# A fused two-block kernel on one core: list stage spread over steps, mask chunks one per two steps, loads and stores over two queues

## The chip, the core and the metric

The kernel runs on one core of a Trainium2 chip. Times are microseconds (us) from the device; the metric is the time of the whole kernel, the median of several runs. Engines: PE is TensorE's matmul, PEld its weight load, DVE is VectorE, ACT ScalarE, POOL GpSimd, SP SyncE. SP, ACT and POOL also issue transfers; their issuing sides stand in the trace as SPq, ACTq and POOLq.

## The reference, cut to what matters

256 tokens with 2048 features pass two transformer-like blocks. What the change touches is the last part, a mixture of 128 x 128 = 16384 single-neuron experts. Every token picks 128 of them (8 heads, 16 each) and weighs them by a gate:

```
z   = einsum('cd,ced->ce', x, u[expert])       # hidden product of token and expert
act = gelu(z) * gate
x   = x + einsum('ce,ced->cd', act, v[expert]) # then a last rms norm
```

## The kernel before, in words

All weights arrive as items of 1 MB (128 partitions x 2048 floats) and are used once. `stream` (line 388) runs over all items in two halves each. For a half it emits: on ScalarE the rounded high part `whi` of a half that lies three halves ahead (`cut_hi`, 416), one call of `step`, on VectorE the rest `wlo` (`cut_lo`, 423; four `wlo` buffers, five `whi`), and the matmuls of the present half. `cut_lo` of an item's second half frees its raw buffer and issues the load of the item three further on, on SP's queue (`load`, 408). Each engine and each queue works in the order in which the program emits.

`step` (347) advances background tasks: of the first three of the list `tasks` each runs to its next `yield`. A yield names a cost; steps get a budget of 1.3 here, debt is carried over, and a task whose cost leaves the credit at or under zero ends the step. In this part each task advances by about one yield per step, with two steps per item.

In the expert part there are 16 items `w_pq` (the choice of experts), 128 items `peer_u` (hidden products with all experts, two items to a PSUM pair), one item `peer_v` by column and 105 gathered items of `peer_v`.

- Scatter (1360): POOL adds the gates one by one into a table `zg` in DRAM, first the first token tile's and then the second's, 256 transfers.
- Hidden products: at the end of a pair `post_u` (1590) copies one part of the PSUM pair on ScalarE (`scaled`, 337), adds the other on VectorE (340), multiplies (341), applies GELU on ScalarE (1594), and stores to the table on ScalarE's queue (1595). All of it is emitted at once behind the pair's last matmul.
- Masks: `mask_task` (1418) waits for item 63 (first token tile) or 96 (second). It reads the tile's gates back from the table in eight chunks of 1 MB on SP's queue (1427), behind the last scatter of that tile, into four buffers `vraw`; VectorE takes the maximum of a chunk (1445); for the second tile POOL halves the chunk first (1438).
- Lists: `list_task` (1457), which follows the second masks, builds a list of the experts in use, of three classes: scans and small matmuls, then 37 pieces in a loop (1556). For a piece POOL compares (`late`, 1516), VectorE makes a selection (`hot`, 1523), TensorE multiplies (1533) into one of two PSUM banks `bg1`, ScalarE takes signs (1542), and VectorE sums them (1548), one iteration apart each. The end (1564 to 1569) makes the indices and sets the flag "lists".
- Rows: items of `peer_v` are loaded by POOL with a gather by index (1649). `cut_lo` asks for them seven items ahead (430), and the first one runs steps until the flag is there:

```
while "lists" not in self.flags:
    self.step()
```

- End: `finish_tile` (1731) scales and stores the 256 x 2048 result in blocks of 512 columns: of the second tile blocks 0 to 2 on VectorE (1746), block 3 on ScalarE and POOL (1748, 1749), and all stores on SP (1750).

At the start `start`, `warm_up` and `prologue` (567 to 610) load the parameters and x in four parts and the first weights, all on SP.

Of the kernel before, what the change touches and what calls it, by code (L numbers as in the profile page):

```python
# [17 lines left out]
P = 128  # L18
# [39 lines left out]
LAST = 3  # L58
U_MASK = (63, 96)
EARLY = 3  # L60
# [187 lines left out]
class Build:  # L248
# [139 lines left out]
    def stream(self, items):  # L388


        n = len(items)
        raw, cut, order = {}, {}, []
        fills = {FILL_FROM + FILL_STEP * j: j for j in range(FILLS)}
# [25 lines left out]
        def cut_lo(k):  # L419
            if k < 2 * n:  # L420
                i, half = order[k]
                lo = self.strm.tile([P, HALF], F32R, name="wlo", tag="wlo", bufs=CUT_BUFS - 1)
                self.V.tensor_tensor(lo, raw[i][:, half * HALF:(half + 1) * HALF], cut[k][0].bitcast(F32),  # L423
                                     op=ALU.subtract)
                cut[k][1] = lo
                if half:
                    del raw[i]
                    if i + RAW_BUFS < n and not callable(items[i + RAW_BUFS][0]):
                        load(i + RAW_BUFS)
                    if i + RAW_BUFS + ROW_BUFS < n and callable(items[i + RAW_BUFS + ROW_BUFS][0]):  # L430
                        load(i + RAW_BUFS + ROW_BUFS)

# [134 lines left out]
    def start(self):  # L567
        nc, A, V = self.nc, self.A, self.V
        cp = self.constp
        self.x = cp.tile([P, KC, TOK], F32, name="xres")  # L570
        self.params = cp.tile([P, PARAM_N], F32, name="params")
        self.cons = {}
        self.ones = cp.tile([P, 1], F32, name="ones")
        self.keys = cp.tile([P, 2, P], F32, name="keys")
        self.decay = cp.tile([P, 2, KC], F32, name="decay")
        V.memset(self.ones, 1.0)
        self.zero = cp.tile([P, 2 * TOK], F32, name="zero")
        self.G.memset(self.zero, 0.0)
        self.warm_up()
        nc.sync.dma_start(self.params, A["params"])  # L580
        self.load_x(0)
        self.act = self.first = Operand(self)

    def warm_up(self):


        zero = self.rowp.tile([P, TOK], F32, name="rstd", tag="rstd", bufs=2)
        self.V.memset(zero, 0.0)
        w = self.strm.tile([P, HALF], F32R, name="wlo", tag="wlo", bufs=CUT_BUFS - 1)
        self.S.activation(w[:, :TOK], zero, AF.Copy)  # L590
        ps = self.bg1()
        for _ in range(WARM):
            self.T.matmul(ps[:, :TOK], w[:, :P], w[:, :TOK], start=True, stop=True)

    def load_x(self, i):
        self.nc.sync.dma_start(self.x[:, 4 * i:4 * i + 4], self.A["xT"][:, 4 * i:4 * i + 4])

    def prologue(self, load):
        load(0, 0, HALF)
        self.load_x(1)  # L600
        load(1, 0, HALF)
        self.load_x(2)
        self.load_x(3)
# [634 lines left out]
    def peer(self):  # L1238
# [144 lines left out]
        def begin_lists():  # L1383
# [17 lines left out]
            for name, (o, w) in offsets.items():  # L1401
                self.cons[name] = c3[:, o:o + w]
            st["abs"], st["gt"] = cut(2, PIECE * P), cut(2, PIECE, P)
            st["hot"], st["prer"] = self.t([2, PIECE * P], "hot", dt=F32R), self.t([PIECE, 3, 130], "pre", dt=F32R)
# [5 lines left out]
            st["zat"], st["vat"], st["over"] = cut(NLIST, dt=U32), cut(NLIST, dt=U32), cut(2, dt=mybir.dt.int32)  # L1410
            st["zg"], st["gates"], st["far2"], st["cd"] = cut(ROWS, 2, TOK), cut(TOK), cut(P + 4), [None, None]
            assert at[0] <= 2 * KC * TOK
# [5 lines left out]
        def mask_task(ti):  # L1418
# [23 lines left out]
            for g in range(8):  # L1442
                load(g + 3)
                half(g + 1)
                V.tensor_reduce(st["m"][:, ti, 16 * g:16 * g + 16], chunks[g], axis=AX.X, op=ALU.max)
                yield 1.25 if ti else 2.3
# [10 lines left out]
        def list_task():  # L1457
# [8 lines left out]
            yield 2.2  # L1466
            yield 0.0
            ps = self.bg1()
            T.matmul(ps[:, 0:3], self.con("tri"), st["n"], start=True, stop=True)
            yield 0.0  # L1470
            far = st["far2"]
            V.tensor_scalar(far[:, 0:3], ps[:, 0:3], -1.0, None, op0=ALU.mult)
# [7 lines left out]
            yield 2.0  # L1480
            yield 0.0
            ps = self.bg1()
# [19 lines left out]
            for c in range(3):  # L1502
# [5 lines left out]
                o += n  # L1508
            yield 1.4

# [26 lines left out]
            def signs(i):  # L1537
                if 0 <= i < len(pieces):
                    c, b, n = pieces[i]
                    col, pv = CLASS_AT[c] + b, banks.pop(i)  # L1540
                    S.activation(st["row"][:, col:col + n], pv[:, 0:n, P], AF.Copy)
                    S.activation(st["gt"][:, i % 2, 0:n], pv[:, 0:n, 0:P], AF.Sign, bias=self.con("past", col, col + 1))

            def sums(i):
                if i >= 0:
                    c, b, n = pieces[i]
                    col = CLASS_AT[c] + b
                    V.tensor_reduce(st["sum"][:, col:col + n], st["gt"][:, i % 2, 0:n], axis=AX.X, op=ALU.add)

            late(0)  # L1550
            late(1)
            yield 0.0
            yield 0.0
            hot(0)
            yield 0.0
# [34 lines left out]
        def post_u(i):  # L1590
            def f(ps):
                z = self.t([2, TOK], "z", 3)
                self.scaled(z, ps)
                S.activation(z, z, AF.Gelu)  # L1594
                d = self.nc.scalar.dma_start(table[:, i:i + 2, 0], z)
                for other in scatters[0] + scatters[1]:
                    self.tc.declare_no_dep(d.ins, other.ins, reason="gates stand beside the hidden products")
                stores.append(d)
            return f

        def post_last(j):

            def f(ps):
                if j == 0:
                    st["zlast"] = self.t([2, TOK], "z", 3)
                z = st["zlast"][:, j]
# [124 lines left out]
        def finish_tile(ti):  # L1731
# [11 lines left out]
            for fb in range(4):  # L1743
# [65 lines left out]
```

## Time and profile before

| | |
|---|---|
| time, median of 3 runs | 2501.93 us (2500.69 to 2504.32) |
| profiled execution | 2507.9 us, its span 2506.1 us |
| mean granted TensorE clock | 0.991 |
| busy | PE 98%, PEld 86%, DVE 71%, ACT 54%, POOL 32% |
| transfers | 548 MB, mean 219 GB/s |

The span is the time from the first to the last instruction of the profiled execution, cut into stretches in microseconds from its start. A granted clock of 1.00 is 2.4 GHz, 0.50 is 1.2 GHz; a value between is a mean over the stretch. The DMA share is the mean busy share of 16 transfer engines and can stand over 1, since packets overlap. In the waits, "A <- B: total, times, longest" says that A's engine sat idle until B.

### The profile page before, as it was taken

Reading aid. Unit: us, or ns where it says so; the run is one execution under the profiler, and the core shown is the slowest. Engines: PE = TensorE matmul, PEld = TensorE weight load, DVE = VectorE, ACT = ScalarE, POOL = GpSimd, SP = SyncE. Lnnn points to the kernel's source line nnn. Section 1 sums busy time; section 2 is a strip of 40 time slices with the busy share of each in tenths; the row PEclk is TensorE's granted clock in tenths of the full one; section 3 lists DMA queues with packets and bytes.
Section 4 is the critical chain, followed back from the end, with each engine's and each line's share of the span. In section 5 each row is a group of like instructions: output and inputs, shape, how many; then the busy total and the mean of one; then the engine's idle time right before and its main releaser. Section 6 shows DMA issues by size and latency. Waiting matters only on the chain.

```text
span 2506.1 us, 37010 instructions
## 1 busy us (share of the span) xinstructions
PE 2447.8 (98%) x14251; PEld 2146.4 (86%) x14251; DVE 1786.4 (71%) x2838; ACT 1342.8 (54%) x1881; POOL 805.0 (32%) x521
## 2 busy tenths in 40 slices
PE   9999999999999999999999999999979899999997
PEld 7888888898888888889999988888867788787885
DVE  7677777777666877766899755575567747777776
ACT  6566555555555677654444544444434535555555
POOL 0000000000000000000688877867523325565553
PEclk9999999999999999999999999999999899999999
DMA  7545555565544565654677777897785468899995
GB/s 251 187 152 173 197 206 202 187 226 185 196 150 165 202 198 186 219 191 170 171 193 196 218 221 208 222 314 223 219 263 189 147 246 299 318 316 320 317 320 183
DMA packets 179925, 548.00 MB, mean 219 GB/s; under 512 B 47585, under 2 KB 113633, under 8 KB 123938
## 3 DMA queue, kind: packets, MB, share of 16 engines
q1 hardware_dynamic: 102082, 391.18, 45.5%
q0 software_dynamic: 60384, 137.79, 19.3%
q10 hardware_dynamic: 17280, 16.65, 1.9%
q8 instruction: 112, 1.84, 0.3%
q14 instruction: 67, 0.55, 0.1%
HBM read 509.77 MB, written 35.78 MB: 218 GB/s over the span
## 4 chain that ended last, share of the span: by engine, by line
PE 84%; issue 4%; DVE 4%; DMA 3%; POOL 2%; ACT 2%; SPq 0%; ACTq 0%; POOLq 0%; DVEq 0%
PE mm L468 38%; PE mm L469 19%; PE mm L460 3%; PE mm L462 3%; PE mm L461 3%; PE bg L1695 2%; PE mm L1695 2%; PE mm L1696 2%; PE bg L1696 2%; PE mm L1694 2%; PE bg L1694 2%; DVE wlo L423 2%; POOL lists L1657 1%; DMA raw<-peer_u 1%; DMA vraw<-zg 1%
## 5 line engine op out<-in xcount | busy, mean ns | idle before, releaser
L468 PE MATMUL mm<-act,whi 128*128 128x512 f32 x4368 | 1228.2, 399 | 8.6 <-ACT whi L416 5.0
L423 DVE TENSOR_TENSOR wlo<-raw,whi 128x1024 fp32r<-128x1024 f32 x754 | 911.9, 1233 | 215.4 <-ACT whi L416 152.7
L468 PEld LDWEIGHTS mm<-act,whi 128*128 128x128 f32 x4368 | 792.9, 190 | 133.4 <-ACT whi L416 6.8
L1360 POOL DMA_INDIRECT zg<-sel,at x256 | 471.4, 1842 | 1316.8 <-DMA raw<-w_pq 1205.2
L416 ACT ACTIVATE whi<-raw 128x1024 fp32r<-128x1024 f32 x754 | 762.0, 1050 | 151.4 <-PE mm L468 37.8
L469 PEld LDWEIGHTS mm<-act,wlo 128*128 128x128 f32 x4368 | 675.7, 191 | 78.0 <-DVE wlo L423 11.5
L469 PE MATMUL mm<-act,wlo 128*128 128x256 f32 x4368 | 702.2, 283 | 8.1 <-DVE wlo L423 7.9
L460 PE MATMUL mm<-act,whi 128*128 128x256 f32 x768 | 218.1, 284 | 0.0
L462 PE MATMUL mm<-act,wlo 128*128 128x256 f32 x768 | 217.5, 283 | 0.2 <-DVE wlo L423 0.2
L461 PE MATMUL mm<-act,whi 128*128 128x256 f32 x768 | 217.3, 283 | 0.0
L337 ACT ACTIVATE z<-mm 128x512 f32<-128x512 f32 x106 | 63.2, 596 | 275.1 <-PE mm L468 275.0
L340 DVE TENSOR_TENSOR z<-z,mm 128x512 f32<-128x512 f32 x106 | 72.8, 686 | 157.4 <-ACT z L337 156.8
L423 DVE TENSOR_TENSOR wlo<-vraw,whi 128x1024 fp32r<-128x1024 f32 x120 | 142.9, 1222 | 40.8 <-ACT whi L416 29.3
L1667 ACT ACTIVATE parts<-lists 128x256 fp32r<-128x256 f32 x105 | 43.9, 418 | 193.2 <-DVE lists L1665 193.2
L462 PEld LDWEIGHTS mm<-act,wlo 128*128 128x128 f32 x768 | 146.9, 191 | 0.5 <-DVE wlo L423 0.4
L461 PEld LDWEIGHTS mm<-act,whi 128*128 128x128 f32 x768 | 147.0, 191 | 0.2
L460 PEld LDWEIGHTS mm<-act,whi 128*128 128x128 f32 x768 | 147.0, 191 | 0.0
L1695 PE MATMUL bg<-wlo,parts 128*128 128x512 f32 x312 | 125.6, 403 | 2.1 <-DVE wlo L423 2.1
L1695 PE MATMUL mm<-wlo,parts 128*128 128x512 f32 x312 | 122.4, 392 | 2.9 <-DVE wlo L423 2.8
L1657 POOL DMA_INDIRECT lists<-zg,lists x105 | 114.4, 1090 | 32.7 <-issue 31.7
L1694 PE MATMUL mm<-whi,parts 128*128 128x512 f32 x312 | 122.4, 392 | 2.2 <-PEq L1714 1.9
L1594 ACT ACTIVATE z<-z 128x512 f32<-128x512 f32 x63 | 39.8, 632 | 157.8 <-DVE z L341 85.4
(344 smaller groups left out, 2687.9 us busy)
## 6 DMA issues: line engine op xcount, KB each, us to landing
raw<-peer_u SPq DMA_DIRECT2D x128, 1024.0 KB
raw<-w_in SPq DMA_DIRECT2D x50, 1024.0 KB
raw<-w_rnn SPq DMA_DIRECT2D x48, 1024.0 KB
zg<-zero SPq DMA_DIRECT2D x16, 1024.0 KB
raw<-w_out SPq DMA_DIRECT2D x16, 1024.0 KB
raw<-w_ple_gate SPq DMA_DIRECT2D x16, 1024.0 KB
raw<-w_q SPq DMA_DIRECT2D x16, 1024.0 KB
raw<-w_o SPq DMA_DIRECT2D x16, 1024.0 KB
```

Source lines behind the costliest of these rows:

```text
L416: self.S.activation(hi, raw[i][:, half * HALF:(half + 1) * HALF], AF.Copy)
L423: self.V.tensor_tensor(lo, raw[i][:, half * HALF:(half + 1) * HALF], cut[k][0].bitcast(F32), op=ALU.subtract)
L460: self.T.matmul(ps, wh, ah, start=first, stop=False)
L461: self.T.matmul(ps, wh, al, start=False, stop=False)
L462: self.T.matmul(ps, wl, ah, start=False, stop=last)
L468: high = lambda i: self.T.matmul(ps, hi[:, ws[i]], both[i], start=(first and i == 0), stop=(last and i == n - 1))
L469: low = lambda i: self.T.matmul(ps[:, 0], lo[:, ws[i]], both[i][:, 0], start=False, stop=False)
L1360: d = G.indirect_dma_start(cells, bass.IndirectOffsetOnAxis(st["at"][:, ti, k:k + 1], 0), st["sel"][:, 2, ti, k:k + 1], None, bounds_check ...
L1657: d = G.indirect_dma_start(st["zg"][:, v % ROWS].rearrange("p n t -> p (n t)"), None, rows, bass.IndirectOffsetOnAxis(st["zat"][:, b:b + 1 ...
L1694: T.matmul(ps, ch[:, ts], hi, start=False, stop=False)
L1695: T.matmul(ps, ch[:, ts], lo, start=False, stop=False)
L1696: T.matmul(ps, cl[:, ts], hi, start=False, stop=last)
```

## The change

- The second mask task starts at item 92 instead of 96. A mask task yields once more per chunk, so a chunk takes two steps.
- Gathered rows that are due before the flag "lists" is set are put off, until it is set or until the row is three items away.
- In the list stage some empty yields go, the first steps are grouped anew, signs and sums come one iteration later, products use four PSUM banks (two `bg1` and the two of `bg2`), and the signs have three buffers. A helper array goes; its place is taken by an existing one.
- The hidden products of a pair become a task at the front of the list, in steps of copy; add and multiply; GELU and store. They use four buffers `z`.
- At the start ScalarE's queue loads x and the parameters, x first; SP loads the weights. The warm-up's copy is VectorE's.
- At the end, for the second tile, the stores of blocks 1 and 3 go on ScalarE's queue.

```diff
-U_MASK = (63, 96)
+U_MASK = (63, 92)
 ...
                     if i + RAW_BUFS + ROW_BUFS < n and callable(items[i + RAW_BUFS + ROW_BUFS][0]):
-                        load(i + RAW_BUFS + ROW_BUFS)
+                        rows.append(i + RAW_BUFS + ROW_BUFS)
+                    while rows and ("lists" in self.flags or rows[0] <= i + RAW_BUFS):
+                        load(rows.pop(0))
 ...
+        self.load_x(0)
+        nc.scalar.dma_start(self.params, A["params"])
+        for i in range(1, 4):
+            self.load_x(i)
         self.warm_up()
-        nc.sync.dma_start(self.params, A["params"])
-        self.load_x(0)
 ...
-        self.S.activation(w[:, :TOK], zero, AF.Copy)
+        self.V.tensor_copy(w[:, :TOK], zero)
 ...
     def load_x(self, i):
-        self.nc.sync.dma_start(self.x[:, 4 * i:4 * i + 4], self.A["xT"][:, 4 * i:4 * i + 4])
+        self.nc.scalar.dma_start(self.x[:, 4 * i:4 * i + 4], self.A["xT"][:, 4 * i:4 * i + 4])
 ...
             for g in range(8):
                 load(g + 3)
                 half(g + 1)
+                yield 0.0
                 V.tensor_reduce(st["m"][:, ti, 16 * g:16 * g + 16], chunks[g], axis=AX.X, op=ALU.max)
                 yield 1.25 if ti else 2.3
 ...
             yield 2.2
-            yield 0.0
             ps = self.bg1()
             T.matmul(ps[:, 0:3], self.con("tri"), st["n"], start=True, stop=True)
 ...
-            yield 1.4
 ...
-            banks = {}
+            banks, more = {}, self.bg2()
 ...
-                    ps = self.bg1()
+                    ps = self.bg1() if i % 4 < 2 else more[:, i % 4 - 2]
 ...
             late(0)
+            yield 1.4
             late(1)
-            yield 0.0
-            yield 0.0
             hot(0)
-            yield 0.0
-            for i in range(len(pieces) + 2):
+            yield 0.6
+            for i in range(len(pieces) + 3):
                 late(i + 2)
                 hot(i + 1)
-                sums(i - 2)
-                signs(i - 1)
+                sums(i - 3)
+                signs(i - 2)
                 products_of(i)
                 yield 1.25
 ...
         def post_u(i):
             def f(ps):
-                z = self.t([2, TOK], "z", 3)
-                self.scaled(z, ps)
-                S.activation(z, z, AF.Gelu)
 ...
+                if i < P - 4:
+                    self.spawn(hidden_task(i, ps), front=True)
+                else:
+                    for _ in hidden_task(i, ps):
+                        pass
             return f
+
+        def hidden_task(i, ps):
+
+            yield 0.0
+            z = self.t([2, TOK], "z", 4)
+            merged = len(ps.shape) == 4
+            if merged:
+                S.activation(z, ps[:, :, 1], AF.Copy)
+                yield 0.0
+                V.tensor_tensor(z, z, ps[:, :, 0], op=ALU.add)
+            V.tensor_tensor(z, z if merged else ps, self.bc2(self.row), op=ALU.mult)
+            yield 0.0
+            S.activation(z, z, AF.Gelu)
+            d = self.nc.scalar.dma_start(table[:, i:i + 2, 0], z)
 ...
-                self.nc.sync.dma_start(A["out"][ti * P:(ti + 1) * P, cs], out[:, cs])
+                (self.nc.scalar if ti and fb % 2 else self.nc.sync).dma_start(A["out"][ti * P:(ti + 1) * P, cs], out[:, cs])
```

## Rows read from the trace of the kernel before

**Rows 1.** The page's first part: busy us, share of the span, instructions.
```profile
PE 2447.8 (98%) x14251; PEld 2146.4 (86%) x14251; DVE 1786.4 (71%) x2838; ACT 1342.8 (54%) x1881; POOL 805.0 (32%) x521
```

**Rows 2.** Line 468 by stretch: length, PE busy (count), PEld, clock, DMA share, GB/s.
```profile
1400.00:1600.00 200.00, 155.25 (x573) 102.85 (x571) 1.00 0.76 216
1600.00:1700.00 100.00, 74.46 (x272) 48.78 (x271) 1.00 0.99 287
1805.00:1870.00 65.00, 39.33 (x136) 26.03 (x135) 0.94 0.92 289
1895.00:2012.00 117.00, 71.17 (x227) 42.98 (x228) 0.91 0.47 160
```

**Rows 3.** Two stretches of all engines: PE, PEld, DVE, ACT, POOL; clock, DMA, GB/s.
```profile
1820.00:1830.00 10.00, 10.00 (x60) 8.81 (x59) 8.30 (x6) 3.87 (x5) 4.80 (x2) 1.00 1.08 331
...
2000.00:2010.00 10.00, 9.33 (x31) 7.86 (x32) 6.84 (x16) 4.03 (x10) 5.19 (x6) 0.54 0.19 52
```

**Rows 4.** SP's issues: weight loads 1230 to 1783 by source; the first second-tile chunk.
```profile
L408 SPq DMA_DIRECT2D raw<-peer_u x96: 327/328/5876, 1238.4 to 1782.7; - x96
...
1805.44 0.43 SPq L1427 DMA_DIRECT2D vraw<-zg  x1
```

**Rows 5.** Waits: who, for whom, us in total, times, longest.
```profile
DVE lists L1445 <- POOL vraw L1438: 12.9, 4, 4.6
...
PE bg L1533 <- ACT lists L1542: 10.2, 6, 1.7
PE bg L1469 <- DVE lists L1465: 5.0, 1, 5.0
```

**Rows 6.** Scatter's line: ns, first and last start; its queue's packets 1791 to 1793.
```profile
L1360 POOL DMA_INDIRECT zg<-sel,at x256: 1546/1556/4850, 1206.4 to 1787.9; - x128
...
q0 software_dynamic: 2, 0.00, 0.0%
```

**Rows 7.** PE in order of time: two neighbouring pieces, start and us.
```profile
1895.67 0.45 PE L1533 MATMUL bg<-pre,hot 128*128 128x130 f32 x3
1898.81 0.45 PE L1533 MATMUL bg<-pre,hot 128*128 128x130 f32 x3
```

**Rows 8.** PE in order of time where pieces stand alone: first and last rows.
```profile
1992.24 0.56 PE L1533 MATMUL bg<-pre,hot 128*128 128x130 f32 x4
...
2003.58 2.87 PE L468 MATMUL mm<-act,whi 128*128 128x512 f32 x6
```

**Rows 9.** Groups by line: busy us, mean ns, then idle time before and its releaser.
```profile
L423 DVE TENSOR_TENSOR wlo<-raw,whi 128x1024 fp32r<-128x1024 f32 x754 | 911.9, 1233 | 215.4 <-ACT whi L416 152.7
...
L337 ACT ACTIVATE z<-mm 128x512 f32<-128x512 f32 x106 | 63.2, 596 | 275.1 <-PE mm L468 275.0
L340 DVE TENSOR_TENSOR z<-z,mm 128x512 f32<-128x512 f32 x106 | 72.8, 686 | 157.4 <-ACT z L337 156.8
...
L1523 DVE SCALAR_TENSOR_TENSOR hot<-lists 128x384 fp32r<-128x384 f32 (+1 forms) x37 | 23.1, 623 | 0.1
L1548 DVE TENSOR_REDUCE lists<-lists 128x3 f32<-128x384 f32 (+1 forms) x37 | 19.2, 522 | 0.2 <-ACT lists L1542 0.2
```

**Rows 10.** The start: ScalarE's first residual part, and a stretch of all engines.
```profile
5.36 1.71 ACT L312 ACTIVATE act<-xres,params 128x256 fp32r<-128x256 f32 x4 [2.92 <-DMA xres<-xT]
...
8.00:12.00 4.00, 3.32 (x16) 2.48 (x17) 3.43 (x6) 3.23 (x8) 0.00 (x0) 1.00 1.01 379
```

**Rows 11.** The end in order of time; last row: ScalarE after issuing a store.
```profile
2498.28 0.69 ACT L1748 ACTIVATE lists<-bg,rc 128x512 f32<-128x512 f32 x1 [1.12 <-DVE rc L325]
2498.29 1.41 DVE L1746 SCALAR_TENSOR_TENSOR lists<-mm,rc,xres 128x512 f32<-128x512 f32 x2
2499.05 1.09 POOL L1749 TENSOR_TENSOR lists<-lists,xres 128x512 f32<-128x512 f32 x1 [1.20 <-ACT lists L1748]
2499.07 2.14 SPq L1750 DMA_DIRECT2D out<-lists  x4
...
1841.91 2.95 ACT L416 ACTIVATE whi<-raw 128x1024 fp32r<-128x1024 f32 x3 [0.46 <-ACT z L1594]
```

More of the change, by code (lines that the diff above doesn't have):

```diff
@@ L391, in stream @@
         n = len(items)
-        raw, cut, order = {}, {}, []
+        raw, cut, order, rows = {}, {}, [], []
         fills = {FILL_FROM + FILL_STEP * j: j for j in range(FILLS)}
@@ L595, in load_x @@
     def load_x(self, i):
-        self.nc.sync.dma_start(self.x[:, 4 * i:4 * i + 4], self.A["xT"][:, 4 * i:4 * i + 4])
+        self.nc.scalar.dma_start(self.x[:, 4 * i:4 * i + 4], self.A["xT"][:, 4 * i:4 * i + 4])
     def prologue(self, load):
         load(0, 0, HALF)
-        self.load_x(1)
         load(1, 0, HALF)
-        self.load_x(2)
-        self.load_x(3)
         load(0, HALF)
@@ L1402, in begin_lists @@
                 self.cons[name] = c3[:, o:o + w]
-            st["abs"], st["gt"] = cut(2, PIECE * P), cut(2, PIECE, P)
+            st["abs"], st["gt"] = cut(2, PIECE * P), cut(3, PIECE, P)
             st["hot"], st["prer"] = self.t([2, PIECE * P], "hot", dt=F32R), self.t([PIECE, 3, 130], "pre", dt=F32R)
@@ L1410, in begin_lists @@
             st["zat"], st["vat"], st["over"] = cut(NLIST, dt=U32), cut(NLIST, dt=U32), cut(2, dt=mybir.dt.int32)
-            st["zg"], st["gates"], st["far2"], st["cd"] = cut(ROWS, 2, TOK), cut(TOK), cut(P + 4), [None, None]
+            st["zg"], st["gates"], st["cd"] = cut(ROWS, 2, TOK), cut(TOK), [None, None]
             assert at[0] <= 2 * KC * TOK
@@ L1470, in list_task @@
             yield 0.0
-            far = st["far2"]
+            far = st["abs"][:, 0]
             V.tensor_scalar(far[:, 0:3], ps[:, 0:3], -1.0, None, op0=ALU.mult)
@@ L1541, in signs @@
                     S.activation(st["row"][:, col:col + n], pv[:, 0:n, P], AF.Copy)
-                    S.activation(st["gt"][:, i % 2, 0:n], pv[:, 0:n, 0:P], AF.Sign, bias=self.con("past", col, col + 1))
+                    S.activation(st["gt"][:, i % 3, 0:n], pv[:, 0:n, 0:P], AF.Sign, bias=self.con("past", col, col + 1))
             def sums(i):
@@ L1547, in sums @@
                     col = CLASS_AT[c] + b
-                    V.tensor_reduce(st["sum"][:, col:col + n], st["gt"][:, i % 2, 0:n], axis=AX.X, op=ALU.add)
+                    V.tensor_reduce(st["sum"][:, col:col + n], st["gt"][:, i % 3, 0:n], axis=AX.X, op=ALU.add)
             late(0)
+            yield 1.4
             late(1)
-            yield 0.0
-            yield 0.0
             hot(0)
-            yield 0.0
-            for i in range(len(pieces) + 2):
+            yield 0.6
+            for i in range(len(pieces) + 3):
                 late(i + 2)
                 hot(i + 1)
-                sums(i - 2)
-                signs(i - 1)
+                sums(i - 3)
+                signs(i - 2)
                 products_of(i)
@@ L1591, in f @@
             def f(ps):
-                z = self.t([2, TOK], "z", 3)
-                self.scaled(z, ps)
-                S.activation(z, z, AF.Gelu)
[L1595 to L1598, printed above, removed]
-            return f
+                if i < P - 4:
[3 more added lines that the diff above has]
+                        pass
+            return f
+        def hidden_task(i, ps):
[10 more added lines that the diff above has]
+            d = self.nc.scalar.dma_start(table[:, i:i + 2, 0], z)
+            for other in scatters[0] + scatters[1]:
+                self.tc.declare_no_dep(d.ins, other.ins, reason="gates stand beside the hidden products")
+            stores.append(d)
+            yield 0.0
         def post_last(j):
@@ L1604, in f @@
                 if j == 0:
-                    st["zlast"] = self.t([2, TOK], "z", 3)
+                    st["zlast"] = self.t([2, TOK], "z", 4)
                 z = st["zlast"][:, j]
```

## Prediction

> **What bounds the kernel now.** I read the page's busy shares first: TensorE is busy for 98% of the span [rows 1], so everything on the other engines counts only where TensorE waits or runs slowly. A busy share can't show that, since a matmul that waits for its clock is busy too; so the next view is the count of one line's matmuls in equal stretches. Line 468 issues eight per half item. Undisturbed it issues 573 in 200 us [rows 2], 0.349 us each, 2.79 us per half item. Against that rate:
> - 1600 to 1700 (mask chunks of the first token tile): 272 x 0.349 = 95.0 us, 5.0 us lost.
> - 1805 to 1870 (mask chunks of the second tile): 136 x 0.349 = 47.5, 17.5 us lost.
> - 1895 to 2012 (list pieces): 227 x 0.349 = 79.2; a step with a piece takes 3.14 us [rows 7] instead of 2.79, so the 37 pieces themselves need 37 x 0.35 = 13.0; 24.8 us lost.
>
> Together 47 us; the change aims at these three. The views of waits and of time say what is late there. In the second mask stretch VectorE sits 12.9 us waiting for POOL's halving of a chunk [rows 5], ahead of weight cuts in its own queue, because a chunk is wanted in every step (all eight are issued within nine steps, the first at 1805.44 [rows 4]) while the transfers run at their ceiling, 331 GB/s at a share of 1.08 [rows 3]. In the list stretch a piece waits 1.7 us for the sign on ScalarE, six times [rows 5], and at its end TensorE does almost only pieces from about 1992 to 2003.6 [rows 8], at a mean clock of 0.54 in the last 10 us [rows 3]: that clock level (1.2 GHz is half of 2.4) follows the gaps.
>
> **Why the pieces bunch up.** A background task advances one yield per step, and there are two steps per item. From item 96 of the peer_u items (step 192) I count 64 steps to the flag "lists": 4 to load, 8 chunks, 1 threshold, 11 of preparation, 39 in the loop over pieces, 1 end. The first row gather asks for the flag with the second half of item 122, at step 242. By then 51 have run; the other 13 are run at once, ten pieces among them.
>
> **The change, part by part.**
> (1) *Mask at 92, flag asked for later, slower chunks.* The start is step 184. Now 4 + 16 (two steps per chunk) + 1 + 7 of preparation + 40 + 1 = 69 steps, the last is step 252. The deferred row gathers ask for the flag with the second half of item 126, at step 250, when 67 have run. Two are forced: the last sum and the conversion to indices, some 2 us of VectorE work and no matmul, covered by the three halves that the cuts run ahead. So the bunch goes. If it stayed at half its size, half of some 12 us would stay.
> (2) *Signs and sums one iteration later, four PSUM banks, third sign buffer, hidden products as a task.* The 1.7 us arise since ScalarE, behind the copy of a finished pair, waits for TensorE and then for VectorE before it comes to the next sign. Split into steps, the copy finds its pair finished, and a bank has two more iterations before it is reused. Per 3.14 us step VectorE has 1.23 for the cut, 0.62 for hot, 0.52 for the sum, and a quarter of a pair's two operations of 0.69 [rows 9]: 2.7 us. It fits, with little to spare. I put the list stretch at 2 us lost instead of 24.8: -22.8 (bounds: -24.8, and -12 if the bunch goes and all six waits, 10.2 us [rows 5], stay).
> (3) *Second mask stretch.* Now two steps of 2.79 us ask for a chunk and an item, 2 x 1.049 MB in 5.58 us = 376 GB/s, still above 331. And something new comes: the chunk loads must wait for the last scatter of the second tile. POOL starts it at 1787.9, and the software queue has two packets left after 1791 [rows 6]. The first chunk would now go behind the 96th weight load, at 1782.7 [rows 4], so SP stands still until about 1792, 9 us, and weight loads 97 and on stand behind it on that queue. TensorE is then ten halves before item 96 (four wlo buffers hold VectorE to that lead): needed by 1782.7 + 27.9 = 1810.6, less 2.3 for the two cuts, so 1808; as second in the queue at 1792 it has 2.1 MB to wait for, 6.4 us: no stall yet. The backlog of 8 chunks, 7 items and about five 256 KB stores is 16.25 x 1.049 = 17.0 MB; at 331 GB/s 51.5 us, so the seventh item lands at 1843.5 to 1845, wanted at 1782.7 + 22 x 2.79 - 2.3 = 1841.8. Some 3 us late. With 3 for the scans, whose matmul now comes one step sooner (it cost 5.0 [rows 5] when VectorE was late), I take 6 us lost instead of 17.5: -11.5. Bounds: 0 lost, and at the mean rate of that stretch, 289 GB/s [rows 2], 59 us of backlog, 9 late, with the full 5.0 some 14 lost.
> (4) *First mask stretch.* Its tile's scatters are long done, its chunks go from 1.77 steps (2.3 of credit against 1.3 per step) to 2: demand falls from 400 to 376 GB/s. 5.0 becomes 4: -1. Bounds -5 and, the ceiling being lower beside the scatters, +2.
> (5) *Hidden products as tasks, elsewhere.* The same instructions, later: the copy two steps, the add three steps after the pair. The bank is wanted again four halves (11.2 us) after the pair's end, and VectorE reaches that add with a lead of about two halves, so some 6 us are left. Nothing, and the bound is the slower rival below.
> (6) *Row gathers four items later.* Five go at once on POOL; the first row is cut five steps later, multiplied eight halves later (over 22 us). Nothing; if they collided, 5 x 1.049 MB at 331 GB/s, 16 us, is the most they could hold.
> (7) *Start.* ScalarE's first residual part waits for x at 5.36, and the transfers are full from there (379 GB/s, share 1.01) [rows 10]. Weights are issued up to 0.9 us sooner, but x now shares the engines with them: 0.524 MB at 379 GB/s, 1.4 us. Bounds -0.9 and +1.4; I take 0, the load being the same. The Trainium skill says in "DMA: Bandwidth & Descriptors" (Issuing engines are not separate DMA queues) that transfers from several engines share the same DMA engines, and a second issuer saves only issue time. The full share in this stretch agrees. By that rule the sum could reach -35 at best, by the 0.9 us of issue; queues with a rate of their own could halve the 2.92 us wait for x besides, for -36.
> (8) *End.* For the second tile ScalarE now issues the store of block 1 ahead of its own block 3. That store waits for VectorE's second block, 2498.29 + 1.41 = 2499.70; with 0.46 us for an issue on ScalarE, block 3 starts at 2500.2 instead of 2498.28, POOL's gain ends near 2502.0 (0.69 + 1.09), and the last store goes then instead of about 2500.9, the last of four SP issues that took 2.14 us from 2499.07 [rows 11]. +1.2 (bounds -0.3, if a queue of its own helps the last landing, and +1.5).
>
> **Sum.** -22.8 - 11.5 - 1 + 0 + 1.2 = -34. The profiled execution took 2507.9 (span 2506.1), 6 us over the median of 2501.93; the stretches are the same work, so I subtract from both: span 2472, time **2468 us**. Own range 2459 to 2479.
>
> **The rivals.**
> - *SP's wait eats the mask gain* (0.20). For: 9 us of standing still ahead of a backlog at the ceiling, 3 us late by my own count. Against: those 22 us of earlier start are longer than 9. The second mask stretch stays at 17.5: 2479.5.
> - *The bunch stays* (0.08): the change does not do what it says. Two tasks of hidden products can be alive at once, and only three tasks advance per step; were the mask task pushed out of a step now and then, more of its 69 steps would be forced. Against: the scatter task and the first mask task are over by item 92. The list stretch stays: 2491.
> - *Slower* (0.04): TensorE waits for a pair's bank. Place: the first matmul of every later pair; price: copy and add, 0.60 + 0.69 us [rows 9], on 50 merged pairs, 64 us: 2532. It outweighs the rest from 0.68 us per pair on. For: add and copy now stand behind two or three cuts. Against: the 6 us in (5), and VectorE is no fuller than 0.6 outside the mask and list stretches.
>
> **How the numbers follow.** The forecast has 0.68. The range reaches from 2457 (all three stretches nearly clean, 45 us off) to 2487, past the first rival and toward the second, and leaves out about 0.15. A measurement of this kernel can't tell less than about 0.2% (5 us) from no change. All cases but the last are faster by more: 0.93; 0.03 for cases that mix the last with the others, 0.04 slower.
>
> **What would show it.** Right: line 468 at about 275 in a 100 us stretch of the second masks, no wait of line 1533's matmuls on the signs, no stretch with only pieces, clock 1.00 from 1400 to the end of the peer_u items, and the last store issued by ScalarE about 1 us later after the last matmul. The wait on SP shows as 9 us without an issue near 1783, with chunks landing late behind it. The forecast is wrong if weight cuts wait for peer_u for more than 10 us in the second mask stretch, if pieces still stand alone before the first row gather, or if the first matmul of a pair waits for VectorE's add.

## The result, and the profile after

The changed kernel takes **2523.34 us**, median of 4 runs (2523.08 to 2524.28), against 2501.49 (2500.69 to 2504.32) for the kernel before: a ratio of 1.008, 95% interval 1.0068 to 1.0092. By that ratio it is 0.8% slower, where 2468 was forecast. The profiled execution took 2524.3 (span 2522.5); that of before lay 6 above its median, so between the two traces 16.4 of the 21.9 us are to be found.

In the changed kernel the main matmul is line 470 (468 before), the scatter 1361 (1360), the chunk load 1428 (1427), POOL's halving 1439 (1438), VectorE's maximum 1447 (1445), the add of the hidden products 1605.

**Where the time is.** The count of the main matmul by stretch, read as in [rows 2], is the first view; here three stretches of the changed kernel:

```profile
L470 PE MATMUL mm<-act,whi x573: 389/393/400, 1399.7 to 1599.5; 128*128 128x512 f32 x191
```

From 1600 to 1700 it issues 209 (272 before), from 1800 to 1905 192 (240), and from 1905 to the end of its work 409 (297). At 0.349 us for each of these matmuls, and 0.35 us for each of the 37 list pieces (in the kernel before three of them lie ahead of 1905), this much time is lost up to the first row matmul (2056.3 before, 2071.8 after):

| us lost | before | after | difference |
|---|---|---|---|
| 1400 to 1600 | 0 | 0 | 0 |
| 1600 to 1700, first masks | 5.1 | 27.1 | +22.0 |
| 1700 to 1800 | 0.2 | 0.9 | +0.7 |
| 1800 to 1905, second masks | 20.2 | 38.0 | +17.8 |
| 1905 to the first row matmul, lists | 35.7 | 11.1 | -24.6 |

That is +15.9 (272 x 0.349 is 94.9 and not the 95.0 of the prediction, so 5.1 stands here for its 5.0). In both kernels the last line holds some 7 us of other matmuls (lines 1688 and 1702), which are work and not loss. The list stretch gave what was forecast for it, and the two mask stretches, which should have got 12.5 us shorter, cost 40 more. The first row matmul itself comes 15.5 us later, with what is left of the later start in it. From there to the last scale (line 325) the changed kernel needs 1.0 us less, 440.8 against 441.8: its granted clock is 1.00 behind the first row matmul, that of the kernel before 0.81 from 2056 to 2065. The end takes 1.85 us more. Together these are the 16.4.

**What is late there.** The waits of both mask stretches ("A <- B: total, times, longest"), first 1600 to 1700, then 1800 to 1900:

```profile
ACT whi L416 <- DMA raw<-peer_u: 50.3, 6, 27.8
DVE lists L1447 <- DMA vraw<-zg: 21.6, 1, 21.6
...
ACT whi L416 <- DMA raw<-peer_u: 64.7, 7, 38.8
DVE lists L1447 <- POOL vraw L1439: 37.6, 2, 35.3
PEld mm L470 <- issue: 34.0, 3, 29.3
PE mm L470 <- DVE z L1605: 33.2, 3, 29.0
```

Weights come late, chunks come late, and TensorE waits for an add that stands in VectorE's queue behind the maximum of a late chunk. Around its two longest waits, 16.0 and 29.0 us, the granted clock is 0.59 (1640 to 1660) and 0.61 (1850 to 1870), and the first matmuls behind them are slow: those of 1863.58 and 1864.01 start 0.43 us apart, those of 1867.24 and 1867.49 0.25. All of it comes through one queue, so SP's own waits are next, 1600 to 1660 and 1780 to 1860:

```profile
SPq L1428 <- DMA zg<-sel,at: 32.2, 1, 32.2
...
SPq L1428 <- DMA zg<-sel,at: 43.4, 1, 43.4
```

Both times SP stands at the first chunk load of a tile until that tile's last scatter has landed, with the weight loads behind it. The timeline of SP shows the hole (start, duration):

```profile
1775.76 28.33 SPq L408 DMA_DIRECT2D raw<-peer_u  x6
1847.53 0.38 SPq L1428 DMA_DIRECT2D vraw<-zg  x1
1848.01 1.72 SPq L408 DMA_DIRECT2D raw<-peer_u  x1
1849.78 6.51 SPq L1428 DMA_DIRECT2D vraw<-zg  x2
```

The first chunk goes at 1847.53 (1805.44 before [rows 4], and 1792 by the forecast). The chain of work that ended last, from 1600 to 1700, names the same culprit:

```profile
by line: POOL zg L1361 52.0%; issue 38.3%; DMA zg<-sel,at 10.9%; POOLq L1361 0.6%
```

**The scatters got slower.** Nothing in the change touches them. Min, median and max in ns, first and last start, to be held against [rows 6]:

```profile
L1361 POOL DMA_INDIRECT zg<-sel,at x256: 1546/2036/5380, 1207.1 to 1844.5; - x128
```

The median went from 1556 to 2036 ns, the sum from 471.4 to 526.5 us, and the last start from 1787.9 to 1844.5: 56.6 us later, of which the sum explains 55.1. Why shows when POOL and VectorE are laid side by side, in a stretch where no mask runs. The changed kernel, the cuts (VectorE, line 423) and then the scatters:

```profile
1441.53 1.23 DVE L423 TENSOR_TENSOR wlo<-raw,whi 128x1024 fp32r<-128x1024 f32 x1 [1.56 <-PE mm L471]
1444.35 1.23 DVE L423 TENSOR_TENSOR wlo<-raw,whi 128x1024 fp32r<-128x1024 f32 x1 [1.59 <-PE mm L471]
1447.13 1.23 DVE L423 TENSOR_TENSOR wlo<-raw,whi 128x1024 fp32r<-128x1024 f32 x1 [1.56 <-PE mm L471]
...
1441.70 2.48 POOL L1361 DMA_INDIRECT zg<-sel,at  x1 [0.30 <-issue]
1444.48 2.51 POOL L1361 DMA_INDIRECT zg<-sel,at  x1 [0.30 <-issue]
1447.30 2.48 POOL L1361 DMA_INDIRECT zg<-sel,at  x1 [0.30 <-issue]
```

The kernel before, in the same order:

```profile
1449.29 3.50 DVE L423 TENSOR_TENSOR wlo<-raw,whi 128x1024 fp32r<-128x1024 f32 x3 [2.21 <-ACT whi L416]
1453.25 1.22 DVE L423 TENSOR_TENSOR wlo<-raw,whi 128x1024 fp32r<-128x1024 f32 x1 [0.46 <-issue]
...
1449.37 2.57 POOL L1360 DMA_INDIRECT zg<-sel,at  x1 [2.82 <-DMA zg<-sel,at]
1452.24 1.97 POOL L1360 DMA_INDIRECT zg<-sel,at  x1 [0.30 <-issue]
1454.51 1.55 POOL L1360 DMA_INDIRECT zg<-sel,at  x1 [0.30 <-issue]
1456.37 1.55 POOL L1360 DMA_INDIRECT zg<-sel,at  x1 [0.31 <-issue]
1458.22 1.55 POOL L1360 DMA_INDIRECT zg<-sel,at  x1 [0.30 <-issue]
```

Read the lengths. A scatter that starts while a cut runs is longer by almost what is left of that cut: at 1444.48 the cut that began at 1444.35 has 1.10 us left, and the scatter takes 2.51 instead of 1.55, 0.96 more. From 1400 on, 119 scatters of the changed kernel start in a cut. 115 of them are longer by what is left of it less 0.13 us, to within 0.04; three meet no more than 0.13 us of it and one starts together with its cut, and these four take 1.55. In the kernel before, the blocking hidden products hold ScalarE at a pair's end, so VectorE's cuts come three at once (3.50 us) and then pause, and scatters of 1.55 follow one another. In the changed kernel ScalarE is not held there, each cut starts as soon as TensorE frees a `wlo` buffer, every 2.79 us, and a lock forms: the held scatter ends 1.42 us after its cut (1444.18 against 1442.76), the next starts 0.30 later, at 1.72, but the next cut starts at 1.59 already. So each scatter starts 0.13 to 0.17 us inside a cut and pays for nearly all of it: 2.79 us per scatter, where 1.85 would do. Counted over the rows of both timelines from 1400 to 1600, with those of two experiments below beside them:

| 1400 to 1600 | scatters | of them started in a cut | longer than 1.55, sum |
|---|---|---|---|
| before | 87 | 34 | 27 us |
| changed | 70 | 66 | 58 us |
| before, tasks alone (experiment 1) | 71 | 66 | 58 us |
| changed, split cuts (experiment 7) | 95 | 34 | 2 us |

**Right as forecast.** In the list stretch no product waits for a sign any more, none stands alone ahead of the first row gather, and the granted clock is 1.00 where it was 0.54 in [rows 3]: here 1990 to 2010 of the changed kernel (busy time and count of each engine, then clock, DMA share, GB/s).

```profile
1990.00:2010.00 20.00, 20.00 (x121) 17.66 (x121) 16.33 (x23) 12.04 (x22) 6.62 (x7) 1.00 0.57 186
```

**Start and end.** ScalarE's table load and its wait changed places against [rows 10]. First the load of the kernel before, then the changed kernel:

```profile
0.73 1.28 ACT L590 ACT_TABLE_LOAD   x1 [0.73 <-PEq L1801]
...
6.18 1.28 ACT L312 ACT_TABLE_LOAD   x1 [6.18 <-DMA xres<-xT]
7.48 1.71 ACT L312 ACTIVATE act<-xres,params 128x256 fp32r<-128x256 f32 x4
...
10.18 1.20 PE L470 MATMUL mm<-act,whi 128*128 128x512 f32 x4 [3.42 <-ACT whi L416]
```

The warm-up's copy was ScalarE's first activation and brought the table in while x was on its way; on VectorE it doesn't, so 1.28 us stand behind x, and the first weight matmul runs at 10.18 instead of 8.07. At the end ScalarE's block 3 stands behind a store that it issues itself, as worked out:

```profile
2514.27 0.35 ACTq L1764 DMA_DIRECT2D out<-lists  x1
2514.67 0.69 ACT L1762 ACTIVATE lists<-bg,rc 128x512 f32<-128x512 f32 x1 [2.97 <-DVE lists L1760]
2515.43 1.09 POOL L1763 TENSOR_TENSOR lists<-lists,xres 128x512 f32<-128x512 f32 x1 [3.04 <-ACT lists L1762]
2516.56 0.34 ACTq L1764 DMA_DIRECT2D out<-lists  x1
```

From the last scale (2512.64) to the end of the span it is 9.86 us; before it was 8.01 (2498.09 to 2506.1).

### The profile page after: what moved, and what is told of

It reads as the page before. It is cut to its first block, busy times and chain, and to the rows that moved or that the text cites. A ratio compares the mean times of both kernels' runs of the same rounds, so it can differ in the third digit from the quotient of the medians.

```text
span 2522.5 us, 37061 instructions
## 1 busy us (share of the span) xinstructions
PE 2436.8 (97%) x14251; PEld 2142.2 (85%) x14251; DVE 1783.0 (71%) x2839; ACT 1347.6 (53%) x1880; POOL 862.4 (34%) x521
## 4 chain that ended last, share of the span: by engine, by line
PE 67%; POOL 14%; issue 11%; DMA 5%; DVE 2%; ACT 1%; POOLq 0%; ACTq 0%; SPq 0%; DVEq 0%
PE mm L470 28%; PE mm L471 14%; POOL zg L1361 12%; PE mm L462 3%; PE mm L463 3%; PE mm L464 3%; DMA zg<-sel,at 2%; PE bg L1709 2%; PE mm L1709 2%; PE mm L1710 2%; DMA raw<-peer_u 2%; PE mm L1708 2%; PE bg L1708 2%; PE bg L1710 2%; DVE wlo L423 1%
## 5 line engine op out<-in xcount | busy, mean ns | idle before, releaser
L470 PE MATMUL mm<-act,whi 128*128 128x512 f32 x4368 | 1229.2, 398 | 63.3 <-DVE z L1605 41.2
L416 ACT ACTIVATE whi<-raw 128x1024 fp32r<-128x1024 f32 x754 | 778.7, 1053 | 502.3 <-PE mm L470 258.1
L1361 POOL DMA_INDIRECT zg<-sel,at x256 | 526.5, 2057 | 1318.3 <-DMA raw<-w_pq 1205.8
L1708 PE MATMUL mm<-whi,parts 128*128 128x512 f32 x312 | 121.8, 390 | 0.4
L1708 PE MATMUL bg<-whi,parts 128*128 128x512 f32 x312 | 121.9, 391 | 0.2
L1710 PE MATMUL bg<-whi,parts 128*128 128x512 f32 x312 | 121.8, 391 | 0.0
L1710 PE MATMUL mm<-whi,parts 128*128 128x512 f32 x312 | 121.4, 389 | 0.0
```

The costliest lines, as they stand in the source:

```text
L416: self.S.activation(hi, raw[i][:, half * HALF:(half + 1) * HALF], AF.Copy)
L470: high = lambda i: self.T.matmul(ps, hi[:, ws[i]], both[i], start=(first and i == 0), stop=(last and i == n - 1))
L1361: d = G.indirect_dma_start(cells, bass.IndirectOffsetOnAxis(st["at"][:, ti, k:k + 1], 0), st["sel"][:, 2, ti, k:k + 1], None, bounds_check ...
L1708: T.matmul(ps, ch[:, ts], hi, start=False, stop=False)
L1710: T.matmul(ps, cl[:, ts], hi, start=False, stop=last)
```

## The experiments

Theory: the hidden products as tasks space the cuts evenly, that locks the scatters to them, and the first chunk load of each tile waits for the scatters. Rivals: TensorE waits for a pair's bank; the earlier masks ask for more than the transfers give; the rest of the change.

**1. Are the tasks enough, and are they needed?** The kernel before with nothing but the tasks (its edit: `hidden_task` and its spawn, as in the change above):

> The kernel before, with nothing changed but the hidden products as a task and a fourth buffer for them. Lock-step theory: scatter mean 2.05, last scatter near 1845, both mask stretches starve (some 27 and 20 us), the bunch of pieces stays: 2515 to 2530. Rival, the start at 92 or the list stage's steps are the cause: scatters as before, the waits of pieces on the signs gone, 2490 to 2500. A bank released later would show as first matmuls of pairs waiting for VectorE's add in undisturbed stretches, several us per 100.

Measured 2527.35, ratio 1.0082 (1.0061 to 1.0102): as much as the whole change loses, from the one edit and without the earlier masks, with the last scatter at 1849.7 and a mean of 2100 ns. The changed kernel with the tasks taken out of the pairs:

```diff
-                if i < P - 4:
+                if i < 0:
```

> The changed kernel, with the hidden products emitted at the pair's end again (not as a task). Lock-step theory (as tasks they even out VectorE's cuts, every scatter then meets one, 2.5 us instead of 1.55, and the masks' loads wait on SP for scatters that end 57 us later): scatter mean back from 2.06 to about 1.85 us, last scatter near 1790, no long gap between SP's issues before the first mask chunks, time 2470 to 2480. Rival, the start at item 92 by itself starves TensorE: the second mask stretch still loses 30 us or more, 2495 to 2510, whatever the scatters take. Rival, the list stage's new steps cost the time: 2515 or more.

Measured 2483.54, ratio 0.9907 (0.9888 to 0.9925), a little above what was expected; last scatter 1790.4, mean 1845 ns. So the tasks cost some 43 us here (0.0173 x 2501.5).

**2. Tasks only when the scatters are done.**

```diff
-                if i < P - 4:
+                if 98 <= i < P - 4:
```

> The changed kernel, with the hidden products as tasks only from pair 98 on, when the scatters should be over, and emitted at the pair's end before that. Lock-step theory: scatters end near 1790, mask stretches lose 5 and 5 to 10 us, list stretch 3 as in the changed kernel: 2466 to 2478. Rival, tasks hurt by a late bank wherever they are: 2480 or more and first matmuls of pairs waiting in the list stretch.

Measured 2471.99, ratio 0.9857 (0.984 to 0.9875). This is what the forecast described: the last scatter at 1792.0, the first chunk on SP soon behind it, and a short wait of SP for it (waits of SP from 1780 to 1860, then its timeline).

```profile
SPq L1428 <- DMA zg<-sel,at: 12.6, 1, 12.6
...
1780.73 2.60 SPq L408 DMA_DIRECT2D raw<-peer_u  x2
1795.93 0.38 SPq L1428 DMA_DIRECT2D vraw<-zg  x1
```

0.0143 x 2501.5 is 35.8 us gained (31 to 40 by the interval); the forecast was 34.

**3. The copy alone at the pair's end**, add and the rest still as tasks:

```diff
-                    self.spawn(hidden_task(i, ps), front=True)
+                    task = hidden_task(i, ps)
+                    next(task)
+                    self.spawn(task, front=True)
...
-            yield 0.0
             z = self.t([2, TOK], "z", 4)
...
-                yield 0.0
+            yield 0.0
+            yield 0.0
+            if merged:
```

> The changed kernel, with only the copy of a pair's first part on ScalarE emitted at the pair's end again; add, multiplication, GELU and store stay in the task. Lock-step theory, with ScalarE's wait for the pair as what bunches the cuts: VectorE's cuts come in threes again, scatter mean 1.85 to 1.95, last scatter before 1805, 2470 to 2488. Rival, VectorE's add and multiplication at their new places slow the scatters: mean stays above 2.0, 2510 or more.

Measured 2491.79, ratio 0.9958 (0.9941 to 0.9974), between the two: ScalarE is held less, the cuts bunch only in part, the mean scatter is 1896 ns and the last starts at 1816.2. The expected time, 2488 at most, was 4 us too low, and the last scatter comes later than the expected 1805.

**4. The cuts in pairs.** In the first 96 items the cut of a first half is put off and emitted beside that of the second:

```diff
-                cut_lo(k + AHEAD)
+                for j in wait:
+                    cut_lo(j)
...
+                wait = [k + AHEAD] if u <= i < u + 96 and half == 0 else []
+                if not wait:
+                    cut_lo(k + AHEAD)
```

> The changed kernel, hidden products still as tasks, but VectorE's cuts of the first 96 peer_u items come two at a time: that of an item's first half is put off by one step and stands right ahead of the second's. Nothing else of the scatters, stores or masks moves. Lock-step theory: in 5.6 us a scatter meets two neighbouring cuts once and has some 2.8 us free, so the mean falls from 2.06 to about 1.85, the last scatter ends before 1805, and 2470 to 2490 results. Rival, the scatters are slowed by transfers or by the stores' new moments: mean stays at 2.05, 2520 to 2530.

Measured 2521.45, ratio 1.0072 (1.0047 to 1.0097): a miss. Its trace shows why it says nothing on the theory: the cuts still come one by one, each waiting for TensorE to free a buffer.

```profile
1441.69 1.23 DVE L423 TENSOR_TENSOR wlo<-raw,whi 128x1024 fp32r<-128x1024 f32 x1 [1.56 <-PE mm L477]
1444.50 1.23 DVE L423 TENSOR_TENSOR wlo<-raw,whi 128x1024 fp32r<-128x1024 f32 x1 [1.59 <-PE mm L477]
...
1441.86 2.48 POOL L1367 DMA_INDIRECT zg<-sel,at  x1 [0.30 <-issue]
1444.64 2.51 POOL L1367 DMA_INDIRECT zg<-sel,at  x1 [0.30 <-issue]
```

The order of emission doesn't space the cuts, the buffers do.

**5. No cuts at all**, for 90 items; the low part of these weights is left out, and the high part is multiplied in its place:

```diff
+                if u <= i < u + 90:
+                    cut[k][1] = cut[k][0]
...
+                    return
```

> The changed kernel, but for the first 90 peer_u items VectorE makes no low part: the matmuls take the high part in its place, so the cut of VectorE is left out there and the output is not the reference's. Scatters, transfers, stores and tasks stay. Lock-step theory (the cut is what a scatter waits for): from 1400 on a scatter takes 1.55 us and 0.30 between two, the last one ends near 1750, the mask loads don't wait, 2462 to 2478. Rival, transfers or stores slow the scatters: mean 2.0 and more as in the changed kernel, 2515 or more.

Measured 2457.32, ratio 0.9822 (0.9806 to 0.9839), mean scatter 1600 ns, the last at 1729.0. The time is 5 us under the expected range. Without cuts nearly every scatter takes 1.55 us, though VectorE still adds and multiplies the hidden products. The time alone says less, since the edit also takes VectorE out of the path of these weights.

**6. The first masks nine items later:**

```diff
-U_MASK = (63, 92)
+U_MASK = (72, 92)
```

> The changed kernel, first mask task from item 72 instead of 63, so that the first tile's scatters are over when its first chunk is wanted. Theory (weights starve on SP behind a chunk load that waits for the scatters): line 470 gets 280 or more in 1600 to 1660, no stall of the first masks beyond 5 us, while the second tile's scatters, no longer sped up by a starving TensorE, end later against the items and the second stretch loses 45 or more; in total 2495 to 2515. Rival, the stall at the first masks is bandwidth, not the wait: it moves to 1660 and later and stays at 25 us or so, time about 2523.

Measured 2523.5, ratio 1.009 (1.0073 to 1.0107). The first stall is gone (286 matmuls from 1600 to 1700), and the second took its time over: SP waits 69.5 us for the scatters, and from 1800 to 1900 there are 104 matmuls (182 in the changed kernel, 287 undisturbed). The last scatter starts at 1843.5, as in the changed kernel. A stall of SP costs by the date on which the scatters end; moving what waits for it moves the stall. The gain that I expected didn't come. The rival's time did, but not its mechanism: there are no stalls between 1660 and 1700, as too many transfers at once would have made.

**7. Each cut in two instructions**, of 512 columns, for the first 98 items. Same work, same tasks, same masks:

```diff
-                self.V.tensor_tensor(lo, raw[i][:, half * HALF:(half + 1) * HALF], cut[k][0].bitcast(F32),
-                                     op=ALU.subtract)
+                u = getattr(self, "base", n) + 16
+                parts = 2 if u <= i < u + 98 else 1
+                for a in range(parts):
+                    q = slice(a * HALF // parts, (a + 1) * HALF // parts)
+                    self.V.tensor_tensor(lo[:, q], raw[i][:, half * HALF:(half + 1) * HALF][:, q],
+                                         cut[k][0][:, q].bitcast(F32), op=ALU.subtract)
```

> After, with each VectorE cut of 1024 columns (1.23 us) of the first 98 items from peer_u made as two instructions of 512 columns (some 0.65 us each). Theory (a scatter that overlaps a cut waits for it, and one scatter is lost to each instant at which a cut runs): a scatter is held only to the end of a half, so a mean scatter falls below 2.0 us (2.06 in after), the last one starts before 1830, and the time is 2490 to 2515. Rival (the scatter pays for the busy time of VectorE, however it is cut): the mean stays at 2.05 or more, the last scatter at 1844 or later, 2520 or more.

Measured 2457.88, ratio 0.9814 (0.9799 to 0.9829), beyond the expectation: mean scatter 1676 ns, the last at 1750.3. The lock is broken although VectorE is busy for longer (1.29 us for two halves instead of 1.23). Experiment 9 has the same cuts, and its timeline, cuts first, shows how:

```profile
1456.04 1.30 DVE L427 TENSOR_TENSOR wlo<-raw,whi 128x512 fp32r<-128x512 f32 x2 [1.52 <-PE mm L475]
1458.83 1.29 DVE L427 TENSOR_TENSOR wlo<-raw,whi 128x512 fp32r<-128x512 f32 x2 [1.49 <-issue]
...
1454.88 1.55 POOL L1366 DMA_INDIRECT zg<-sel,at  x1 [0.30 <-issue]
1456.73 2.03 POOL L1366 DMA_INDIRECT zg<-sel,at  x1 [0.30 <-issue]
1459.07 1.88 POOL L1366 DMA_INDIRECT zg<-sel,at  x1 [0.30 <-issue]
1461.25 1.62 POOL L1366 DMA_INDIRECT zg<-sel,at  x1 [0.30 <-issue]
```

The scatter of 1459.07 starts in a first half that ends near 1459.52 and is held 0.33 us only, though the second half follows at once. It is held to the end of the instruction that it meets and not again. From 1400 on this goes for all 46 scatters of experiment 7 that start in one half with more than 0.13 us of it left. Before 1400, where the choice of experts still runs on VectorE, eight were held through both halves (the one of 1268.49 had 0.26 us left and took 0.73 longer); why is open.

The same edit in the kernel before:

> Before, with the same split of the cuts of the first 98 items from peer_u into two instructions of 512 columns. Theory (in before nothing waits for the scatters, since its second masks start with item 96, at 1805, behind the last scatter at 1788): the mean scatter falls from 1.84 to about 1.7 us and the last one starts near 1750, but the time stays within 0.3% of before, 2495 to 2510; the early end of the scatters is worth something only together with the earlier masks. Rival (the hold of POOL and VectorE on each other costs before as well, in its own mask stretches): 2480 or less.

Measured 2509.11, ratio 1.0011 (1.0001 to 1.002); mean 1717 ns, the last scatter at 1754.9, 33 us earlier than before, and nothing gained. There nothing waits for the scatters; their end has a price only once the masks come sooner.

**8. Start and end alone**, added to the kernel before (the lines of the change in `start`, `load_x`, `warm_up` and `finish_tile`):

> Before, with only the start and the end of the change (first loads split over SP and ScalarE, last output stores over ScalarE and SP), the steps of the list stage left as in before. Terms read from the trace of after: 0.7 to 1.9 us at the start and 1.9 at the end, so 2.5 to 4 us slower than before, a ratio of 1.001 to 1.0015; the table load of ScalarE stands behind the wait for x, and the last store is issued 3.9 us after the last scale. Rival (both are hidden, or the end of after is its own): within 1 us of before, the last issue 2.8 us after the last scale.

Measured 2507.77, ratio 1.0015 (1.0006 to 1.0024), 3.8 us for both terms together (1.5 to 6.0 by the interval); the counts of [rows 2] are 273, 134 and 230 here where they were 272, 136 and 227. The last issue comes 3.93 us after the last scale, as in the changed kernel. Experiment 2 with start and end put back was to show the same:

> The kernel with tasks from pair 98 on (the fastest so far), with the start's loads, the warm-up copy and the last stores put back to what they were before the change. Both were a loss by the trace of the changed kernel: ScalarE's table load now stands behind the wait for x (first matmul of weights 10.18 instead of 8.07), and the last store goes 1.1 us later after the last scale factor. Expected: 2 to 4 us faster than that kernel on the same footing, ratio to the kernel before 0.984 to 0.986; if start and end are hidden or equal, 0.9855 to 0.987.

Measured 2469.98, ratio 0.9873 (0.9857 to 0.989), outside both expected ranges and above the 0.9857 of experiment 2, whose interval it overlaps: it shows no gain. Its trace does end 8.0 us behind the last scale, as before.

**9. The best of it:** the split cuts of experiment 7, start and end as before.

> After, with the split cuts and with start and end put back as in before: the best of the runs so far (2457.9, ratio 0.9814) less the 2.5 to 4 us of start and end, 2453 to 2456, a ratio near 0.980; span to end 8.0 us behind the last scale. Rival (start and end are worth nothing together with the rest): 2457 to 2459.

Measured **2454.74**, ratio 0.9791 (0.9777 to 0.9804): 2.1%, some 52 us, under the kernel before, from a change that as it stood cost 22. Line 474 is its main matmul; the counts of 1600 to 1700 and the scatters:

```profile
L474 PE MATMUL mm<-act,whi x286: 389/395/400, 1599.7 to 1699.8; 128*128 128x512 f32 x143
...
L1366 POOL DMA_INDIRECT zg<-sel,at x256: 1546/1548/5587, 1207.6 to 1751.5; - x128
```

From 1400 to its first row matmul it loses some 10 us, against 61 in the kernel before (the first table) and 77 in the changed one; in each some 7 are the other matmuls named there.

The order of all runs by the start of the last scatter is nearly that of their times, where the masks are early: 1729 to 1752 gives 0.979 to 0.982, 1790 to 1792 gives 0.986 to 0.991, 1816 gives 0.996, 1842 to 1844 gives 1.007 to 1.009. With the masks as before, 1788 and 1755 give 1 and 1.001, and 1850 gives 1.008.

## Why the prediction was wrong

**The step that failed is (5)**, "Hidden products as tasks, elsewhere. The same instructions, later", priced at "Nothing". The instructions of the tasks were free, as it said. What it left out is what the blocking code had done for others: by holding ScalarE it bunched VectorE's cuts, and the pauses were where the scatters ran at 1.55 us. I looked at who waits for the moved instructions, and not at which engine's rhythm they set. The trace of before had the sign of it in [rows 6], which I quoted: minimum and median of the scatters 1546 and 1556 ns, but a mean of 1842 (471.4 us over 256). The 0.3 us between them went unasked; the timeline above answers it.

**(3) and (4) stood on it.** (3) took the last scatter at 1787.9 from the kernel before and priced SP's wait at 9 us, (4) said that the first tile's scatters are long done. In the kernel before the last of these (the 176th of the 256, since 48 of the second tile's go in between) starts at 1596.25, only 23 us ahead of the chunk load at 1618.97; in the changed kernel it starts at 1643.21. SP waits 43.4 and 32.2 us. Where the scatters end as before (experiment 2), it waits 12.6 and not at all, 12 us are lost in the second mask stretch by the count from 1785 to 1880, where 6 were forecast inside bounds of 0 to 14, and 4.7 in the first, where 4 were.

**The first rival** had the place right and the mechanism half: SP's wait ahead of the second masks. Its price, and with it the chance that the time goes up, was worked out from the scatters of before.

**The slower rival is refuted as a cause**; that its 2532 lies near the measured time is chance. TensorE does wait for line 1605, 41.2 us in all, but that add stands behind a maximum whose chunk is late. With the same tasks and the same banks, and the scatters quick (experiment 7), the main matmul is issued at the full rate from 1600 to 1800, 286 and 287 in 100 us.

**(1) and (2) held**: -22.8 forecast, -24.6 by the table; the bunch is gone and so are the six waits.

**(6)** shows no wait in the changed kernel: the first row matmul follows the one before it at once, where the kernel before waits 1.9 us. **(7) and (8)**, 0 and +1.2, were 3.8 together in experiment 8. (8) was mis-sized: 1.85 for 1.2, above its bound of 1.5. (7) missed the table load: I weighed the order of the loads and not what the copy that goes to VectorE had done on ScalarE besides copying. The first matmul is 2.1 us late; by the first scatter 0.7 of it are left in the trace.

**The sum** of the parts that were forecast (-34) comes out within 2 us once the scatters keep their pace (-35.8), but that is luck in part. Against the kernel before, experiment 2 loses 8 us less from 1785 to 1880, where 11.5 less were forecast, and 28 less from 1880 to the first row matmul, where 22.8 were forecast for the list stretch. What the sum left out was worth some 56 us, 0.0223 x 2501.5 between the changed kernel and experiment 2.

## What to carry to other kernels

When a change turns blocking work into spread steps, its own instructions are the smaller part: ask which engine was held by the block, what ran in the pauses that this made for others, and compare that stretch's timeline engine by engine. Where an operation's median lies well under its mean, find out what the long ones overlap before taking its end as fixed. And when an early consumer is moved up to a producer's end, the producer's pace becomes part of the path: here the same split of a cut was worth nothing in the kernel before and some 66 us in the changed one (0.0266 x 2501.5).

## What the runs showed of the hardware

- A scatter that POOL starts while VectorE subtracts two tensors in SBUF is held until that one instruction ends: 1.55 us become 2.5 beside a cut of 1.23 us, 1.88 or 2.03 beside halves of some 0.69. From 1400 on the hold is what is left of the instruction less 0.13 us, in 115 scatters of the changed kernel and 46 of experiment 7; eight before 1400 in experiment 7 were held longer. One in progress isn't held by an instruction that starts later (before, the scatter of 1449.37 runs on through the second and third of three cuts).
- The multiplication of the hidden products, also with two inputs in SBUF, holds a scatter too: 0.07 us where 0.20 of it were left (10 of 11 times in experiment 7). Started in an add with one input in PSUM (12 times there, 0.4 us of the add left) a scatter took 1.55, and so it did in a maximum with one input in SBUF of which 2.0 us were left.
- The Trainium skill states in "SBUF — State Buffer" (Who interferes with whom) that VectorE with two SBUF inputs contends with a GpSimd instruction that reads SBUF, and that the port pair which the two engines share is an exclusive lock. The holds above agree. The same section infers that such a two-input operation doesn't stall GpSimd's making of descriptors; for these indirect transfers the traces say otherwise, 1.55 against 2.5 us. Which port or read it is, no run here shows.
- Two loops with periods of 1.85 and 2.79 us locked to one another: held to a cut's end, the scatter came out 0.13 us too late for the gap, so that 66 of 70 started in a cut from 1400 to 1600.
